# Loading the projection's weight units from GpSimd's queue, and clearing the inverse's operand on VectorE

## The chip, the cores and the metric

The kernel runs on one core of a Trainium2 chip. The metric is the device time of one execution in microseconds (us); lower is better. The engines are called as in the profile: PE (TensorE, with PEld for its weight loads), DVE (VectorE), ACT (ScalarE), POOL (GpSimd), SP (SyncE, which here only issues DMAs).

## The reference

One layer of a hybrid decoder over 1024 tokens of width 1024, in float32:

```
x = x + 0.5 * swiglu(rms_norm(x))                     # width 2816
h = rms_norm(x);  proj = h @ w_in                     # all projections of the mixer
q, k, v = silu(causal_dwconv(proj[qkv]))              # 8 heads of 128
o_gdn   = rms_norm(gated_delta_rule(q, k, v, g, beta)) * silu(z)
o_ssm   = rms_norm(ssd_scan(...) * silu(z))           # 16 heads of 64
x = x + concat(o_gdn, o_ssm) @ w_out
x = x + 0.5 * swiglu(rms_norm(x));  return rms_norm(x)
```

The gated delta rule works on chunks of the tokens. For each chunk it needs the inverse of a unit lower triangular matrix, I + tril(beta * k k^T * decay), and then steps a 128x128 state through the chunks, head by head.

## The kernel before

All large products are made of float32 numbers split into a rounded part (hi) and a rest (lo), three matmuls for each product: hi*hi, hi*lo and lo*hi, on tiles of 128x128 by 128x512. Most of them also go through a scheme of seven products for a 2x2 block product, in place of eight.

The program runs through the first feed-forward block, the norm, the state-space heads, the eight delta-rule heads, the output projection, and the second feed-forward block. The change lies in the delta-rule heads. Heads 0 to 3 take their projections of q, k, v and z as plain products (`proj_half`). Heads 4 to 7 take them from the scheme of seven products: `chunk` computes two projections of 128 columns for all 1024 tokens from seven weight units, two chunks per head, 8 chunks and 56 units in all. The constant `NESTED = 4` is where the first kind ends, so there are four heads of the second kind.

A weight unit is a tile of 128 partitions x 2 (hi, lo) x 512 float32, 512 KB. The units were computed during the first feed-forward block and stored in DRAM, in `wu_scr`. `first_units` makes four slots in SBUF and loads the first four units; `unit_prod` uses the next unit for twelve matmuls (L1260, L1261, L1262) and then calls `unit_load` for the unit four places on, which goes to the slot just used. That load (L1251) must wait until PE has finished with the slot.

Beside the chunks, each head goes through its own chain:

- `decays` (L1361 to L1370) loads the head's decay row, broadcast over the partitions, from `g_scr` to `dt` (L1365); ACT takes an exponential for `qe` (L1366); POOL masks `dt` causally with an affine select (`causal`, L970); ACT takes eight exponentials of `dt` (L1369).
- `k_part` transposes k on PE (L1346) and makes `kd` and the norms on ACT (L1350, L1355).
- PE multiplies k by k and k by q (L1443, L1444), DVE makes `u` and `dt` of it (L1447, L1450), and `u`'s diagonal 32x32 blocks go to DRAM (L1459) and come back as `fu`, one block per partition row (L1486).
- `token_sums` sums q's squares over the channels on PE (L978), copies the row on ACT (L981) and stores it (L983). Its tile `row` has the same buffer as `fx`.
- `fx` starts as the identity, cleared and set on POOL (L1490, L1492). DVE inverts the blocks by 31 steps of two instructions (L1496, L1498).
- `fx` goes to DRAM (L1501) and back (L1508, L1509). DVE transposes it (L1510), and small matmuls (L1516 to L1542) join the 32x32 blocks to 64x64 and 128x128. For that, the operand `x64` needs a zero block of 32 partitions x 8 x 32 numbers (L1527); the rest of it is written by ACT (L1528 to L1530). `x64` lies in the buffer of `fu`, so it can be written only after the last of the 31 steps.
- The recurrence over the 8 blocks of tokens (L1549 to L1576), the norm (L1582 to L1587), and the store to `mix_scr` (L1588).

The source is written with tiles, and the tool that builds the program adds the waits and decides in which order each engine and each DMA queue gets its instructions, from estimates of when each will be ready. So the trace shows one head's recurrence among the next head's unit products, and the source's order is not that of the trace. Each engine, and each queue, then works in that fixed order, so an instruction that waits holds those behind it.

At the end of the last head, POOL's queue also loads the first operands of the output projection (`out_start`, L1233 and L1234) and stores z (L1428).

Of the kernel before, what the change touches and what calls it, by code (L numbers as in the profile page):

```python
# [11 lines left out]
F32 = mybir.dt.float32  # L12
# [32 lines left out]
def kernel(  # L45
# [6 lines left out]
    nc = tc.nc  # L52
    V, A, G, T = nc.vector, nc.scalar, nc.gpsimd, nc.tensor
# [20 lines left out]
    wu_scr = [dram.tile([P, 7, 2, 512], F32, name=f"wu_scr{i}") for i in range(2 * (GH - 4))]  # L74
# [1171 lines left out]
    def unit_load(s):  # L1246

        if s < 7 * len(wu_scr):
            c, i = divmod(s, 7)
            u = slots[s % 4]  # L1250
            nc.sync.dma_start(out=u.bitcast(F32), in_=wu_scr[c][:, i])  # L1251
            units.append((s, u))

    def unit_prod(bank, m, first):

        s, u = units.pop(0)
        bh, bl = H_IN[m]
        for k in range(4):
            wh, wl = (u[:, i, k * P:(k + 1) * P] for i in range(2))
            T.matmul(bank, lhsT=wh, rhs=bh[k], start=first and k == 0, stop=False, skip_group_check=True)  # L1260
            T.matmul(bank, lhsT=wh, rhs=bl[k], start=False, stop=False, skip_group_check=True)  # L1261
            T.matmul(bank, lhsT=wl, rhs=bh[k], start=False, stop=k == 3, skip_group_check=True)  # L1262
        unit_load(s + 4)
# [48 lines left out]
    def first_units():  # L1312

        for i in range(2):
            t = wp.tile([P, 2, 2, 512], F32R, name="wunits", tag="wst")
            slots.extend(t[:, j] for j in range(2))
        for s in range(4):
            unit_load(s)
# [15 lines left out]
    with ExitStack() as cg:  # L1334
# [37 lines left out]
        for h in range(GH):  # L1372
# [63 lines left out]
            u = g2.tile([P, NB, P], F32, name="u")  # L1436
# [68 lines left out]
            x64, mt2 = lv2[0:64, 0], lv2[:, 1]  # L1505
# [18 lines left out]
                T.matmul(px[64:96, ls], lhsT=mt[96:128, b], rhs=xd[96:128, b], start=True, stop=True)  # L1524
                T.matmul(px[32:64, ls], lhsT=xd[32:64, b], rhs=mt[32:64, b], start=True, stop=True)
            pxv = px[:, 0:256].rearrange("p (b l) -> p b l", b=NB)
            G.memset(x64[0:32, :, 32:64], 0.0)  # L1527
            A.copy(out=x64[0:32, :, 0:32], in_=xtr[0:32])  # L1528
            A.copy(out=x64[32:64, :, 32:64], in_=xtr[32:64])
            A.mul(out=x64[32:64, :, 0:32], in_=pxv[32:64], mul=-1.0)  # L1530
# [227 lines left out]
```

## Time and profile before

| | |
|---|---|
| median of three runs | 2296.49 us (2296.11 to 2296.8) |
| profiled execution | 2296.6 us, of which 2294.9 is the span of the profile |
| granted clock of PE | 0.998 of full speed |
| PE busy | 2257.9 us, 98% of the span |
| DVE, ACT, POOL busy | 76%, 51%, 2% |
| weight units: loaded | 1105.7 to 1409.4 us, 56 loads of 512 KB from SP's queue |
| weight units: multiplied | 1183.2 to 1420 us |

A row of a stretch gives the busy time of each engine in it. A row of waits has the waiting engine, the line that waits, what ended the wait, the total in us, how often, and the longest. SPq and POOLq are the sequencers of the two engines that issue DMAs. In a timeline, the numbers in front are the start from the beginning of the span and the time it took, in us; in brackets stands the idle time of the engine before it and what ended that.

### The profile page before, as it was taken

Reading aid. Unit: us, or ns where it says so; the run is one execution under the profiler, and the core shown is the slowest. Engines: PE = TensorE matmul, PEld = TensorE weight load, DVE = VectorE, ACT = ScalarE, POOL = GpSimd, SP = SyncE. Lnnn points to the kernel's source line nnn. Section 1 sums busy time; section 2 is a strip of 40 time slices with the busy share of each in tenths; the row PEclk is TensorE's granted clock in tenths of the full one; section 3 lists DMA queues with packets and bytes.
Section 4 is the critical chain, followed back from the end, with each engine's and each line's share of the span. In section 5 each row is a group of like instructions: output and inputs, shape, how many; then the busy total and the mean of one; then the engine's idle time right before and its main releaser. Section 6 shows DMA issues by size and latency. Waiting matters only on the chain.

```text
span 2294.9 us, 31984 instructions
## 1 busy us (share of the span) xinstructions
PE 2257.9 (98%) x11654; PEld 1842.1 (80%) x11654; DVE 1751.5 (76%) x3225; ACT 1178.9 (51%) x2276; POOL 52.1 (2%) x118
## 2 busy tenths in 40 slices
PE   7999999999999999999999999999999999999998
PEld 5788888888878878888887777788878888888886
DVE  7989987769776887667667777778688676766787
ACT  7444433354366986875755566523543333334344
POOL 0000000000000110100000000000000000000000
PEclk9999999999999999999999999999999999999999
DMA  3467663497654433242356566436123232329446
GB/s 112 137 217 256 230 214 114 166 333 228 206 180 137 134 120 101 74 132 65 84 158 183 166 175 195 136 99 220 65 88 133 92 119 88 120 89 347 143 151 215
DMA packets 262194, 356.96 MB, mean 156 GB/s; under 512 B 60808, under 2 KB 167404, under 8 KB 260244
## 3 DMA queue, kind: packets, MB, share of 16 engines
q1 hardware_dynamic: 261220, 352.20, 47.2%
q0 software_dynamic: 816, 2.72, 0.3%
q8 instruction: 91, 1.49, 0.3%
q14 instruction: 67, 0.55, 0.1%
HBM read 249.34 MB, written 105.52 MB: 155 GB/s over the span
## 4 chain that ended last, share of the span: by engine, by line
PE 87%; ACT 6%; DVE 5%; issue 1%; DMA 1%; POOL 0%; SPq 0%; DVEq 0%; POOLq 0%; ACTq 0%
PE ps_pj L125 7%; PE ps_pj L123 7%; PE ps_pj L124 7%; PE ps_pj L335 6%; PE ps_pj L334 6%; PE ps_pj L336 6%; PE ps_mx L334 3%; PE ps_mx L336 3%; PE ps_mx L335 3%; PE ps_pj L564 2%; PE ps_pj L565 2%; PE ps_pj L563 2%; PE ps_pj L1260 2%; PE ps_oo L335 2%; PE ps_pj L1261 2%; PE ps_oo L334 2%
## 5 line engine op out<-in xcount | busy, mean ns | idle before, releaser
L336 PE MATMUL ps_pj<-bh,al 128*128 128x512 f32 x688 | 268.1, 390 | 0.0
L335 PE MATMUL ps_pj<-bl,ah 128*128 128x512 f32 x688 | 267.9, 389 | 0.0
L334 PE MATMUL ps_pj<-bh,ah 128*128 128x512 f32 x688 | 267.7, 390 | 0.0
L123 PE MATMUL ps_pj<-hhi,whi 128*128 128x512 f32 x576 | 229.4, 398 | 0.4 <-ACT gsb L901 0.4
L125 PE MATMUL ps_pj<-hhi,wlo 128*128 128x512 f32 x576 | 229.4, 398 | 0.0
L124 PE MATMUL ps_pj<-hlo,whi 128*128 128x512 f32 x576 | 228.3, 396 | 0.0
L336 PEld LDWEIGHTS ps_pj<-bh,al 128*128 128x128 f32 x688 | 129.2, 188 | 26.7
L335 PEld LDWEIGHTS ps_pj<-bl,ah 128*128 128x128 f32 x688 | 129.2, 188 | 26.6
L334 PEld LDWEIGHTS ps_pj<-bh,ah 128*128 128x128 f32 x688 | 129.0, 188 | 26.7
L317 DVE TENSOR_TENSOR as<-wst 128x512 f32<-128x512 f32 x220 | 144.3, 685 | 2.1 <-DMA wst<-in_ffn_w_up_dram 2.0
L241 ACT CAST hid<-hraw 128x1024 fp32r<-128x1024 f32 (+1 forms) x84 | 82.2, 980 | 123.9 <-PE ps_oo L565 46.3
L241 ACT CAST ah<-wst 128x512 fp32r<-128x512 f32 x88 | 54.5, 621 | 176.4 <-PE ps_oo L335 113.4
L242 DVE TENSOR_TENSOR al<-as,ah 128x512 fp32r<-128x512 f32 x220 | 141.1, 685 | 4.8 <-ACT ah L241 4.3
L334 PE MATMUL ps_mx<-bh,ah 128*128 128x512 f32 x352 | 138.6, 396 | 3.9 <-ACT m L343 1.3
L335 PE MATMUL ps_mx<-bl,ah 128*128 128x512 f32 x352 | 138.3, 393 | 0.5 <-DVE bl L242 0.5
L336 PE MATMUL ps_mx<-bh,al 128*128 128x512 f32 x352 | 137.8, 391 | 0.3 <-DVE al L242 0.3
L241 ACT CAST ah<-as 128x512 fp32r<-128x512 f32 x220 | 125.1, 618 | 24.1 <-DVE as L317 24.1
L125 PEld LDWEIGHTS ps_pj<-hhi,wlo 128*128 128x128 f32 x576 | 108.3, 188 | 21.9 <-issue 0.9
L123 PEld LDWEIGHTS ps_pj<-hhi,whi 128*128 128x128 f32 x576 | 108.4, 188 | 21.8 <-ACT gsb L901 0.8
L124 PEld LDWEIGHTS ps_pj<-hlo,whi 128*128 128x128 f32 x576 | 108.4, 188 | 21.1 <-issue 0.8
L242 DVE TENSOR_TENSOR hid<-hraw,hid 128x1024 fp32r<-128x1024 f32 (+1 forms) x84 | 95.0, 1131 | 26.3 <-ACT hid L241 26.1
L343 ACT COPY m<-ps_pj 128x512 f32<-128x512 f32 x88 | 51.4, 587 | 111.7 <-PE ps_pj L336 111.4
(505 smaller groups left out, 5635.4 us busy)
## 6 DMA issues: line engine op xcount, KB each, us to landing
hraw<-hid_scr SPq DMA_DIRECT2D x70, 512.0 KB, 3.9
wu_scr<-wunit SPq DMA_DIRECT2D x112, 256.0 KB, 3.6
wunits<-wu_scr SPq DMA_DIRECT2D x56, 512.0 KB, 3.8
hid_scr<-hs SPq DMA_DIRECT2D x110, 256.0 KB, 2.9
wst<-in_ffn_w_down_dram SPq DMA_DIRECT2D x50, 512.0 KB, 4.7
wst<-in_ffn_w_gate_dram SPq DMA_DIRECT2D x22, 1024.0 KB, 6.0
wst<-in_ffn_w_up_dram SPq DMA_DIRECT2D x22, 1024.0 KB, 6.0
hid_scr<-sg SPq DMA_DIRECT2D x44, 256.0 KB, 2.0
```

What stands on the lines that cost most here:

```text
L123: T.matmul(o, lhsT=wh, rhs=mh, start=first, stop=False)
L124: T.matmul(o, lhsT=wh, rhs=ml, start=False, stop=False)
L125: return T.matmul(o, lhsT=wl, rhs=mh, start=False, stop=last)
L241: return (A.copy(out=hi, in_=src), V.tensor_tensor(out=lo, in0=src, in1=hi.bitcast(F32), op=ALU.subtract))
L242: V.tensor_tensor(out=lo, in0=src, in1=hi.bitcast(F32), op=ALU.subtract))
L317: V.tensor_tensor(out=t, in0=v[0], in1=v[1], op=v[2])
L334: T.matmul(bank, lhsT=wh[:, k], rhs=bh[:, k], start=a, stop=False, skip_group_check=True)
L335: T.matmul(bank, lhsT=wh[:, k], rhs=bl[:, k], start=False, stop=False, skip_group_check=True)
L336: T.matmul(bank, lhsT=wl[:, k], rhs=bh[:, k], start=False, stop=z, skip_group_check=True)
L343: A.copy(out=t, in_=bank)
L563: T.matmul(bank, lhsT=hh, rhs=wh, start=first and k == 0, stop=False, skip_group_check=True)
L564: T.matmul(bank, lhsT=hh, rhs=wl, start=False, stop=False, skip_group_check=True)
```

## The change

Two lines. The load of a weight unit is issued by GpSimd (`G`) in place of SyncE, and the zero block of `x64` is written by VectorE (`V`) in place of GpSimd. Nothing else in the source differs.

```
@@ unit_load
             u = slots[s % 4]
-            nc.sync.dma_start(out=u.bitcast(F32), in_=wu_scr[c][:, i])
+            G.dma_start(out=u.bitcast(F32), in_=wu_scr[c][:, i])
             units.append((s, u))
@@ the head's inverse, L1527
             pxv = px[:, 0:256].rearrange("p (b l) -> p b l", b=NB)
-            G.memset(x64[0:32, :, 32:64], 0.0)
+            V.memset(x64[0:32, :, 32:64], 0.0)
             A.copy(out=x64[0:32, :, 0:32], in_=xtr[0:32])
```

More of the change, by code (lines that the diff above doesn't have):

```diff
@@ L1250, in unit_load @@
             u = slots[s % 4]
-            nc.sync.dma_start(out=u.bitcast(F32), in_=wu_scr[c][:, i])
+            G.dma_start(out=u.bitcast(F32), in_=wu_scr[c][:, i])
             units.append((s, u))
@@ L1526 @@
             pxv = px[:, 0:256].rearrange("p (b l) -> p b l", b=NB)
-            G.memset(x64[0:32, :, 32:64], 0.0)
+            V.memset(x64[0:32, :, 32:64], 0.0)
             A.copy(out=x64[0:32, :, 0:32], in_=xtr[0:32])
```

## The prediction

> **What bounds the kernel now.** I read the page first, its engine totals and the chain that ended last, and then the table of stretches for the place that the change touches.
>
> ```profile
> span 2294.9 us, 31984 instructions
> ...
> PE 2257.9 (98%) x11654; PEld 1842.1 (80%) x11654; DVE 1751.5 (76%) x3225; ACT 1178.9 (51%) x2276; POOL 52.1 (2%) x118
> ...
> PE 87%; ACT 6%; DVE 5%; issue 1%; DMA 1%; POOL 0%; SPq 0%; DVEq 0%; POOLq 0%; ACTq 0%
> ```
>
> ```profile
> 1183.00:1420.00 237.00, 235.84 (x1637) 186.49 (x1635) 168.73 (x546) 140.36 (x398) 8.64 (x29) 1.00 0.61 182
> 1420.00:1440.00 20.00, 17.71 (x77) 13.21 (x76) 14.70 (x23) 19.02 (x38) 2.69 (x3) 1.00 0.40 117
> ```
>
> PE is 87% of the chain that ended last, and SP's and POOL's queues are 0%. In the stretches the columns are the stretch, its length, and the busy time of PE, PEld, DVE, ACT and POOL, then the granted clock (full). The weight units are multiplied from 1183 to 1420. PE idles there for 237.00 - 235.84 = 1.16 us and for 2.29 us in the next 20. The change can win back 3.45 us of idle PE before 1440, no more, unless it also alters how densely PE works while it counts as busy. Who ends this idle time stands in the list of waits of PE, for 1183 to 1460:
>
> ```profile
> PE ps_pj L123 <- ACT xa L1220: 2.3, 2, 2.0
> PE ps_mx L1443 <- ACT kd L1355: 0.8, 2, 0.4
> PE ps_sc L1516 <- DVE lv L1510: 0.2, 1, 0.2
> ```
>
> None of the three is a weight unit, and none is the memset of L1527.
>
> **Part 1: 56 loads leave SP's queue.** SP is often late with them. The waits of SP's queue, 1090 to 1530:
>
> ```profile
> SPq L1251 <- PE ps_pj L1262: 57.0, 21, 6.7
> SPq L1365 <- PE ps_oo L1565: 41.3, 5, 20.5
> SPq L1588 <- ACT vr L1587: 32.2, 6, 19.9
> SPq L1501 <- DVE fx L1498: 28.0, 7, 8.1
> SPq L1251 <- PE ps_pj L1260: 22.2, 6, 4.8
> SPq L983 <- ACT row L981: 20.0, 4, 6.8
> ```
>
> L1251 is the unit load, which waits for the products that still read its slot. The other rows name their own data: the store L1501 waits for fx itself, L983 for its row. So they would not go out sooner with the loads out of the way, and freeing SP gives nothing on them. What does get late is a load behind L983. The worst place that I found, in order of time:
>
> ```profile
> 1320.51 0.55 SPq L983 DMA_DIRECT2D row_scr<-row  x1
> 1321.15 0.39 SPq L1251 DMA_DIRECT2D wunits<-wu_scr  x1
> ```
>
> ```profile
> 1328.94 0.40 PE L1260 MATMUL ps_pj<-hhi,wunits 128*128 128x512 f32 x1
> ```
>
> This product is the first to read the load of 1321.15 (the 34th of 56; units are used in order, twelve products each). Between them are 7.79 us. From issue to landing:
>
> ```profile
> wunits<-wu_scr SPq DMA_DIRECT2D x56, 512.0 KB, 3.8
> ...
> z_scr<-zc SPq DMA_DIRECT2D x7, 512.0 KB, 2.6
> ...
> nat<-ssm_scr SPq DMA_DIRECT2D x3, 1024.0 KB, 4.9
> ...
> y<-ssm_scr POOLq DMA_DIRECT2D x1, 1024.0 KB, 6.0
> x<-in_w_out_dram POOLq DMA_DIRECT2D x1, 1024.0 KB, 10.1
> z_scr<-zc POOLq DMA_DIRECT2D x1, 512.0 KB, 5.2
> ```
>
> 7.79 - 3.8 leaves 3.99 us to spare even there. Loads that go out on time have much the same, where the products of units run back to back, as in these two first products of neighbouring units:
>
> ```profile
> 1295.35 0.39 PE L1260 MATMUL ps_pj<-hhi,wunits 128*128 128x512 f32 x1
> ...
> 1298.08 0.39 PE L1260 MATMUL ps_pj<-t,wunits 128*128 128x512 f32 x1
> ```
>
> A unit takes 2.73 us. With four slots, three units lie between a slot's release and its next use, 8.2 us, and 8.2 - 3.8 is 4.4. So about 4 us is the least, and coming sooner saves zero.
>
> **Part 2: the same loads enter POOL's queue.** Their landing gets slower. From one kind of buffer (ssm_scr, 1024 KB), POOL needs 6.0 and SP 4.9 us, +1.1; for the store of z it is 5.2 against 2.6, +2.6. Those are the two ends, 4.9 and 6.4 us for a unit; I take +1.1, since y is a load from DRAM as the units are. The spare time of 4.0 becomes 2.9 (1.4 at the far end), so PE does not wait. If a load came later than that, PE would stand for the difference, because its products run in a written order.
>
> What is POOL's issue worth, and what waits behind it? The rows of POOL's timeline:
>
> ```profile
> 1298.01 1.09 POOL L970 TENSOR_SCALAR_AFFINE_SELECT dt<-dt 128x1024 f32<-128x1024 f32 x1 [34.24 <-ACT qe L1366]
> ...
> 1322.27 0.32 POOL L1490 MEMSET fx<- 128x256 f32 x1 [20.67 <-DMA row_scr<-row]
> 1322.65 0.58 POOL L1492 MEMSET fx<- 32x8 f32 x4
> ...
> 1405.22 0.58 POOL L1234 DMA_DIRECT2D y<-ssm_scr  x1 [22.37 <-PE ps_oo L1565]
> ```
>
> A load costs POOL about 0.58 us (y), 56 of them 32 us, on an engine that is 8.64 us busy in those 237: room is there. The order is what matters. Three things of POOL are in the way of loads or the other way round. (a) The clearing of fx, L1490, waits for row_scr to land, since the row lies in the same buffer; a load queued behind it goes out at 1322.65 + 0.58 = 1323.2, against 1321.15 now if it is that same load. 3.99 - 2.1 - 1.1 = 0.8 us is then left; at the +2.6 end PE would stand 0.7 us. (b) y and x, from 1405 on, stand ahead of the last loads and fill the queue with 2 MB; in bytes the total is that of before, and the last unit has always shared the engines with them. I take zero, with 0 to 2 us. (c) The causal mask L970 may stand behind a load. That is a wait which before could not exist, and it is the chain of the head: ACT waits for the mask before its eight exponentials.
>
> ```profile
> 1299.13 2.45 ACT L1369 ACTIVATE dt<-dt,ngc 128x128 f32<-128x128 f32 x8 [1.24 <-POOL dt L970]
> ```
>
> Behind the exponentials ACT makes kd, and PE's L1443 is the one that waits for it (0.8 us in two times, above). So that chain has no slack, and whatever the mask loses, PE loses. A load that is due costs the mask its 0.58 us. I put in one such, in one of the three heads whose masks fall among the loads: +0.6 us. The ends are 0 and rival A's price.
>
> **Part 3: the memset goes from POOL to VectorE.**
>
> ```profile
> L1527 POOL MEMSET lv<- 32x256 f32 x8 | 2.4, 302 | 96.8 <-DVE ft L1496 94.6 <-DMA wunits<-wu_scr 2.2
> ```
>
> ```profile
> L1519 DVE COPY lv<-ps_sc x16: 417/424/431, 1064.8 to 1518.1; 32x256 f32<-32x256 f32 x16
> ```
>
> ```profile
> 1301.27 0.17 DVE L1498 TENSOR_TENSOR fx<-fx,ft 128x8 f32<-128x8 f32 x1
> 1301.36 0.68 DVE L1270 TENSOR_TENSOR zc<-ps_pj,zc 128x512 f32<-128x512 f32 x1
> 1302.67 1.29 DVE L847 SCALAR_TENSOR_TENSOR vt__11963<-pre,cols,vt__11963 128x1024 f32<-128x1024 f32 x1 [0.63 <-ACT vt__11963 L1293]
> ```
>
> On POOL it takes 0.30 us; DVE's copy of the same size takes 0.42, which bounds it above. Eight of them are 2.4 to 3.4 us of DVE. It must come behind the last step of fx (1301.27 here), and 0.7 us later DVE itself stands for 0.63 us waiting for ACT, so it is covered. Without that cover 0.4 us in each of the four later heads would fall on u and the next inverse, 1.7 us in all. I take 0. For POOL the removal matters: this memset waits for DVE (94.6 us in all) and would have held the loads.
>
> **The sum.** Against the profiled execution, span 2294.9 and time 2296.6: 0 (SP) + 0 (landing) + 0.6 (mask) + 0 (memset) = 2297.2; its time is 0.1 above the median of the three runs (2296.49), so against that median 2297.1 us. That is within 0.2%, 4.6 us, about the least that a measurement of this kernel can tell from no change.
>
> [...] Two rows of VectorE's timeline:
>
> ```profile
> 1298.13 1.00 DVE L1498 TENSOR_TENSOR fx<-fx,ft 128x24 f32<-128x24 f32 x1
> ...
> 1405.70 0.22 DVE L1498 TENSOR_TENSOR fx<-fx,ft 128x69 f32<-128x69 f32 x1
> ```
>
> The first, 24 elements wide, takes 1.00 us: it lies under the mask of 1298.01. The second, 69 wide, lies under the issue of y (1405.22 + 0.58) and takes 0.22. So POOL's mask holds DVE; a DMA issue does not, and I charge DVE nothing. [...]
>
> **The rivals.**
> A (slower): the queue order holds the mask. If a load stands ahead of it whose slot PE has not yet left, the mask waits for the rest of that unit and the issue. 2.73 us a unit plus 0.58 is 3.3 us per head; in two of the three heads 6.6, so 2303. It decides from the point where the held time passes 2.3 us a head in two heads. For it: the mask (1298.01) and the end of a unit (1298.08) coincide, so the order is a toss. Against: the list that orders the queues places an instruction when it is expected to be ready, which mostly puts a due mask first.
>
> [...]
>
> C (faster): the order changes for the better. Loads that come on time let the products be placed otherwise among the small matmuls:
>
> ```profile
> L1262 PE MATMUL ps_pj<-hhi,wunits 128*128 128x512 f32 x128 | 52.8, 413 | 0.0
> ```
>
> ```profile
> L565 PE MATMUL ps_pj<-wd,hid 128*128 128x512 f32 x37 | 14.5, 392 | 0.0
> ```
>
> The second is the same product away from the heads (600 to 700). 672 products at up to 21 ns are 14 us hidden in busy time. A fifth of it, 2.8, with two thirds of the 3.45 us of idle time, 2.3, gives 2291.4. Against: the switches between large and small matmuls are there in any order.
>
> D (the change does not do what it says): the loads are late as before, held by fx's clearing instead of L983. With 0.8 us to spare it costs nothing, 2296.5, and it is counted in the forecast.
>
> **How the numbers follow.** Forecast with D 0.60 (its own range 2293 to 2300: plus and minus the 3.45 us of idle time), A 0.20, B 0.03, C 0.17. Half of A's nominal cases lie under 2303. Low 2291 leaves out half of C, high 2303 half of A and B: together 0.20. Faster by over 0.2%: C, 0.17. Slower: A and B with 0.02 of the forecast's edge, 0.25. The rest, 0.58, is the same.
>
> **What would show it.** Right: PE idle from 1183 to 1440 between 2.5 and 5 us; L1251 under POOLq with landings near 5 us; SP's waits without L1251, yet L1501 and L1365 as long as now; PE's waits without wunits. Wrong: PE waiting for a DMA wunits<-wu_scr (landing or fx's clearing missed), the mask released by a load rather than by qe, or a stretch whose PE count per us has changed (C).

## The result and the profile after

The changed kernel takes 2317.66 us (median of 4 runs, 2316.76 to 2322.1); the kernel before, on the same chip, 2296.64 us. The ratio is 1.0094, with a 95% interval of 1.0076 to 1.0111: 21 us slower. The forecast was 2297.1 us, in a range that ended at 2303. The profiled execution took 2318.34 us, its span is 2316.6, 21.7 us more than before.

The page of the changed kernel: span, busy engines, and the chain that ended last.

```profile
span 2316.6 us, 31991 instructions
...
PE 2266.9 (98%) x11654; PEld 1850.2 (80%) x11654; DVE 1755.4 (76%) x3233; ACT 1183.3 (51%) x2280; POOL 77.9 (3%) x166
...
PE 74%; DVE 12%; ACT 6%; DMA 4%; issue 2%; SPq 1%; POOL 0%; DVEq 0%; ACTq 0%
```

POOL has 56 loads more to issue and is still nowhere on the chain. What moved there is VectorE: 5% before, 12% now, while PE fell from 87 to 74%. The stretches of the changed kernel (length, busy time of PE, PEld, DVE, ACT and POOL, then granted clock, DMA share, GB/s):

```profile
1183.00:1420.00 237.00, 227.43 (x1592) 180.51 (x1591) 158.84 (x490) 132.61 (x383) 32.83 (x74) 0.99 0.57 162
1420.00:1440.00 20.00, 16.94 (x76) 13.24 (x75) 18.98 (x66) 17.67 (x32) 3.40 (x5) 1.00 0.89 316
1440.00:1460.00 20.00, 18.53 (x150) 14.45 (x149) 13.14 (x27) 16.78 (x35) 0.56 (x1) 0.91 0.35 96
```

PE's idle time from 1183 to 1460 was 3.44 us and is 9.57 + 3.06 + 1.47 = 14.1. And the granted clock, 1.00 there before, is below 1: in three spells (stretches of the clock's record at half of full speed), of 6.83, 3.41 and 10.24 us, PE gets half of it. So there are 10.7 us more of idle time, and PE is busy for 3.79 + 3.41 + 10.24 = 17.4 us of those spells, which costs half of that, 8.7 us (in the second spell, successive 128x512 products of L123 to L125 start 0.43 us apart, just ahead of it 0.23). Together 19.4 us. Against its own matmuls in the trace of before, PE falls back by 18.6 us between 1187 and 1552, so these two account for the loss in this stretch. The rest of the 21.7 us is mostly a lag of 2.9 us that this trace has already at 1187, ahead of the stretch; other traces are there between 1.0 us ahead of before (sp_new_order below, in the same new order) and 2.6 us behind it. The waits of PE from 1183 to 1460, those of 0.9 us and more:

```profile
PE ps_pj L1260 <- DVE pre L1270: 7.2, 2, 5.6
PE ps_pj L124 <- DVE w L242: 2.0, 1, 2.0
PE ps_sc L1516 <- DVE lv L1510: 1.3, 2, 0.8
PE ps_sc L1523 <- DVE lv L1519: 0.9, 1, 0.9
PE ps_pj L123 <- DVE zc L1270: 0.9, 1, 0.9
```

No weight unit is among them. PE waits for VectorE, in lines that the change does not touch. The largest wait is one stall of 5.6 us. ScalarE, VectorE and PE ahead of it in the changed kernel, in their own timelines:

```profile
1227.37 2.45 ACT L1369 ACTIVATE dt<-dt,ngc 128x128 f32<-128x128 f32 x8 [0.23 <-POOL dt L970]
1229.72 1.14 ACT L1293 ACTIVATE kt<-pre,cols 128x1024 f32<-128x1024 f32 x1
...
1239.81 0.59 ACT L1279 COPY pre<-ps_pj 128x512 f32<-128x512 f32 x1 [7.44 <-DVE fx L1498]
```

```profile
1233.29 1.28 DVE L847 SCALAR_TENSOR_TENSOR kt<-pre,cols,kt 128x1024 f32<-128x1024 f32 x1
...
1238.42 1.28 DVE L847 SCALAR_TENSOR_TENSOR kt<-pre,cols,kt 128x1024 f32<-128x1024 f32 x1
...
1239.96 1.15 DVE L847 SCALAR_TENSOR_TENSOR qt<-pre,cols,qt 128x1024 f32<-128x1024 f32 x1
1241.04 0.67 DVE L1270 TENSOR_TENSOR pre<-ps_pj,zc 128x512 f32<-128x512 f32 x1
```

```profile
1241.76 0.79 PE L1260 MATMUL ps_pj<-t,wunits 128*128 128x512 f32 x1 [5.63 <-DVE pre L1270]
```

Read it backwards. PE's product goes into a buffer of `ps_pj` that VectorE's addition L1270 has to read first (1241.04), and stood 5.63 us for that. That addition writes `pre`, which the last of the key's three convolution steps, L847, still reads until 1238.42 + 1.28 = 1239.70 (ScalarE's copy L1279, which also writes `pre`, starts then too; its row names the fx step beside it). And in VectorE's order the addition stands behind the last step of the query as well (1239.96), so it starts at 1241.04. These six steps come last among VectorE's steps of the inverse. Their first input, L1293, comes on ScalarE behind eight exponentials, but it is done at 1230.86, 2.4 us before the first of them, so it is VectorE's own order that holds them. The same instructions in the kernel before:

```profile
1220.78 1.15 ACT L1293 ACTIVATE kt<-pre,cols 128x1024 f32<-128x1024 f32 x1 [3.13 <-DVE pre L1270]
```

```profile
1222.20 1.28 DVE L847 SCALAR_TENSOR_TENSOR kt<-pre,cols,kt 128x1024 f32<-128x1024 f32 x1
```

L1293 stood 9 us earlier there, ahead of L1587, and L847 11 us earlier, among the inverse's steps (2.9 us of each are the lag of the whole trace). What differs is the order that the tool which builds the program wrote for ScalarE, VectorE and PE. The first differences are small: on ScalarE near 1123 us `kd` (L1355) goes behind two copies (L1528, L1529), on VectorE near 1209 us L1471 goes ahead of L1556. From there much of four heads is laid out otherwise: with the two traces aligned from 1100 to about 1620 us, some 315 of VectorE's 1021 instructions, 168 of ScalarE's 726 and 755 of PE's 3327 stand elsewhere, while PE's first 6254 matmuls (to 1228 us) keep their order. That the tool's estimates shift with the loads on another queue is an inference; the estimates are not on record.

### The profile page after: what moved, and what is told of

Same layout as the page of the kernel before. It is cut to its first block, busy times and chain, and to the rows that moved or that the text cites. A ratio compares the mean times of both kernels' runs of the same rounds, so it can differ in the third digit from the quotient of the medians.

```text
span 2316.6 us, 31991 instructions
## 1 busy us (share of the span) xinstructions
PE 2266.9 (98%) x11654; PEld 1850.2 (80%) x11654; DVE 1755.4 (76%) x3233; ACT 1183.3 (51%) x2280; POOL 77.9 (3%) x166
## 4 chain that ended last, share of the span: by engine, by line
PE 74%; DVE 12%; ACT 6%; DMA 4%; issue 2%; SPq 1%; POOL 0%; DVEq 0%; ACTq 0%
PE ps_pj L125 6%; PE ps_pj L124 6%; PE ps_pj L123 6%; PE ps_pj L334 6%; PE ps_pj L336 6%; PE ps_pj L335 6%; PE ps_mx L334 3%; PE ps_mx L336 3%; PE ps_mx L335 3%; PE ps_oo L334 2%; PE ps_oo L336 2%; PE ps_oo L335 2%; PE ps_pj L564 1%; PE ps_pj L565 1%; DMA wst<-in_ffn_w_down_dram 1%
## 5 line engine op out<-in xcount | busy, mean ns | idle before, releaser
L123 PE MATMUL ps_pj<-hhi,whi 128*128 128x512 f32 x576 | 229.4, 398 | 0.7 <-ACT pre L1392 0.4
L125 PE MATMUL ps_pj<-hhi,wlo 128*128 128x512 f32 x576 | 229.2, 398 | 0.0
L123 PEld LDWEIGHTS ps_pj<-hhi,whi 128*128 128x128 f32 x576 | 108.3, 188 | 22.6 <-ACT gsb L901 0.8
L125 PEld LDWEIGHTS ps_pj<-hhi,wlo 128*128 128x128 f32 x576 | 108.3, 188 | 21.9 <-issue 0.9
```

Of the source, the lines that this page charges most:

```text
L123: T.matmul(o, lhsT=wh, rhs=mh, start=first, stop=False)
L125: return T.matmul(o, lhsT=wl, rhs=mh, start=False, stop=last)
```

## Experiments

Theory: the *order* costs the time. Moving the loads made the builder write another one, it stalls PE on VectorE, and the stalls pull the clock down. Rivals: the queue itself costs it (GpSimd's issue and landing), or the clearing on VectorE does. Ratios are to the kernel before on the same chip, with 95% intervals. The last columns compare the profiled execution with that of before (span 2294.9): what the span grew, and how much idle time of PE and half of the time at half clock grew between 1183 and 1500 us, summed from the matmul and clock records. The kernel before ran at 2298.72 us beside the first four runs below the changed kernel, at 2297.48 and 2299.06 beside the next three and the last three, against 2296.64 in the result; expectations in us are to be read with that.

| run | loads | order | median us | ratio | span | idle | clock |
|---|---|---|---|---|---|---|---|
| changed kernel | POOL | new | 2317.66 | 1.0094 [1.0076, 1.0111] | +21.7 | +10.7 | +10.2 |
| load_only | POOL | new | 2318.11 | 1.0079 [1.0056, 1.0101] | +26.1 | +11.1 | +17.1 |
| memset_only | SP | before's | 2300.84 | 1.0006 [0.9996, 1.0016] | -0.4 | +0.3 | 0 |
| pool_old_order | POOL | before's | 2301.23 | 1.0012 [1.0003, 1.0022] | +1.0 | +0.8 | 0 |
| sp_new_order | SP | new | 2314.64 | 1.0063 [1.0045, 1.0080] | +16.5 | +9.0 | +12.0 |
| after_old_order | POOL | before's | 2301.68 | 1.0018 [1.0009, 1.0026] | +10.5 | +2.3 | +6.8 |
| after_taps_early | POOL | new, 20 us of it as before | 2322.83 | 1.0109 [1.0095, 1.0124] | +22.3 | +11.8 | +12.0 |
| before_taps_late | SP | before's, 20 us of it new | 2305.35 | 1.0035 [1.0023, 1.0047] | +6.5 | +5.7 | +1.7 |
| pe_old_order | POOL | before's on PE alone | 2315.88 | 1.0087 [1.0062, 1.0112] | +20.1 | +11.8 | +5.1 |
| dve_act_old_order | POOL | before's on DVE and ACT alone | 2302.24 | 1.0015 [1.0005, 1.0024] | +4.7 | +2.0 | +1.7 |
| act_loads | ACT | a fourth one | 2321.56 | 1.0115 [1.0082, 1.0147] | +22.3 | +15.3 | +8.5 |

Idle time and clock add up to the growth of the span within 5 us in every row (the worst is sp_new_order, 21.0 for 16.5). The column of the clock counts idle time in a spell a second time. With half of PE's busy time in the spells in its place, the two come within 2.3 us of what PE falls back by between 1187 and 1552 in every row (19.9 for 19.0 in sp_new_order).

**Each half of the change alone.** The diffs are its two lines, one at a time.

> The kernel before with the unit loads on GpSimd's queue, and the clearing left on GpSimd. The written order of TensorE, ScalarE and SyncE is that of the changed kernel, instruction for instruction. Order theory (the move of the load makes the program builder write another order for TensorE, VectorE and ScalarE, and that order stalls TensorE): 2316 to 2320 us, PE idle of about 14 us between 1183 and 1460 us, the stall of about 5.6 us ahead of a product of L1260 near 1236 us, three more half-clock spells. Queue theory (GpSimd's queue itself costs it): about 2317 us too. Clearing theory (the eight clears on VectorE cost it): 2296 to 2298 us.

> The kernel before with the clearing alone on VectorE (8 instructions of 0.27 us); the loads stay on SyncE, and TensorE, ScalarE and SyncE keep before's order. Order theory and queue theory: 2295.5 to 2298 us, no more than 8 x 0.27 = 2.2 us above before. Clearing theory: 2317 us.

The load carries all of it (2318.11 us; idle 13.1 us between 1183 and 1460, a first stall of 5.5 us, four spells at half clock in place of the three expected). The clearing alone ran at 2300.84 us, above the 2295.5 to 2298 expected, but so did the kernel before in these rounds: it is 2.1 us over that, with an interval that includes zero, and PE's order is that of before. The clearing theory is dead; order and queue are still together.

**Queue and order taken apart.** Edges of issue order between successive instructions of one engine, with no wait in them, hold PE, VectorE, ScalarE and SyncE to a given order through the nested heads (a cut from the added lines, shortened where the dots stand):

```
+def hold_order(nc, tc):
+    at = {i.name: i for i in nc.cur_bb.bb.instructions}
+    for row in ...:                     # one engine's order, by the numbers of the traced instructions
+        ...
+        tc.add_manual_dep(ins, prev.name, mybir.DependencyInfo(
+            mybir.DependencyClass.NoSync, mybir.DependencyReason.DATA), reason="held order")
```

> The unit loads on GpSimd's queue and the clearing on GpSimd, as in the run with the load alone, but the order in which TensorE, VectorE, ScalarE and SyncE issue their instructions through the nested heads is held to that of the kernel before (edges of issue order only, no waits). Order theory: 2294 to 2299 us, PE idle between 1183 and 1460 us near 3.5 us, one half-clock spell near 1681 us and the one at the end. Queue theory: about 2317 us.

> The unit loads on SyncE's queue and the clearing on GpSimd, as before, but TensorE, VectorE and ScalarE (and SyncE's other transfers) issue in the order of the changed kernel through the nested heads. Order theory: 2314 to 2322 us, with the stall of about 5.6 us near 1236 us and the extra half-clock spells of the changed kernel. Queue theory: 2296 to 2299 us.

With the loads on GpSimd in before's order, all 11654 matmuls come in the order of before, and PE's waits from 1183 to 1460 are those of before:

```profile
PE ps_pj L123 <- ACT xa L1220: 2.9, 2, 2.0
PE ps_mx L1443 <- ACT kd L1355: 0.7, 2, 0.4
PE ps_sc L1516 <- DVE lv L1510: 0.2, 1, 0.2
```

With the loads still on SyncE and the clearing on GpSimd, but in the new order, they are those of the changed kernel:

```profile
PE ps_pj L1260 <- DVE pre L1270: 6.5, 2, 5.0
PE ps_pj L124 <- DVE w L242: 2.1, 1, 2.1
PE ps_sc L1523 <- DVE lv L1519: 0.9, 1, 0.9
```

So the order costs the time without the queue (+0.63%), and the queue without the order costs 0.12%, barely off zero. Its 2301.23 us are 2 us above what I expected (2294 to 2299) and 2.5 above the kernel before in these rounds. Where those lie stays open: its trace, from the fastest of its ten runs, shows 1.0 us more of span and 0.8 of idle time. The sum of the two is 0.75%, under the 0.94% of the whole change, but the intervals are too wide to say whether anything is left.

**The whole change in the old order.** The changed kernel with before's order held in the same way.

> The whole change (unit loads on GpSimd's queue, clearing on VectorE), with TensorE, VectorE, ScalarE and SyncE held to the order of the kernel before through the nested heads. Order theory: 2295 to 2300 us, at most 0.2% from before; PE idle of 3.4 to 4.5 us between 1183 and 1460 us, no extra half-clock spell. If queue and clearing cost something only together: above 2302 us.

2301.68 us, 0.18% over before: within the 0.2%, a little above the microseconds that I expected (the kernel before ran 0.8 us higher here than at the result), and just under the 2302 from which I would have said that queue and clearing cost something together. PE's idle time between 1183 and 1460 is 5.8 us, above the 3.4 to 4.5 expected. Its profiled execution was the slowest of its 12 (2307.16, the fastest 2298.06) and has a spell of 13.65 us at half clock that was not expected; the section on the hardware shows what stands ahead of it.

**Where in the order?** First the 20 us around the largest stall: in the changed kernel, the instructions read above go back to where before has them, and the converse. PE keeps the order of the kernel that each is made from. The moves, in short (`+` marks what goes ahead; taps are the steps of the convolution):

```
 ACT: +L1293 kt, L1587 x8, L1366, +L1293 qt, +L1274, L1369 x8     (taps early; taps late is the reverse)
 DVE: the six L847 and two L1270 among the fx steps of 1224 to 1235, not behind those of 1233 to 1241
```

> The changed kernel with its own order, except in one stretch of 20 us (1222 to 1242): ScalarE's first step of the key's and the query's convolution (L1293) goes ahead of L1587 and L1369, and VectorE's six convolution steps (L847) and two additions (L1270) go where the kernel before has them among the inverse's steps. Stall-and-clock theory (the late steps make the 5.6 us stall, and the stall makes the half-clock spell behind it): the stall near 1236 us falls below 1 us, the spell of 6.8 us at half clock goes with it, in all 5 to 9 us less than the changed kernel: 2309 to 2313 us. If the clock falls for another reason: the stall goes and the spell stays, 2312 to 2314 us. If the stall only moves to a later wait: 2316 to 2318 us.

> The converse: the kernel before, loads on SyncE and clearing on GpSimd, its own order but for the same stretch, in which ScalarE's L1293 and VectorE's convolution steps and additions come as late as in the changed kernel. Stall-and-clock theory: a stall of 5 to 9 us ahead of a product of L1260 near 1233 us and a half-clock spell of 3.4 to 6.8 us behind it: 2303 to 2310 us. If the late steps are not the cause, or other order hides them: 2296 to 2299 us.

Taps late, two stalls of PE appear in before's order:

```profile
1230.42 0.50 PE L1260 MATMUL ps_pj<-hhi,wunits 128*128 128x512 f32 x1 [2.21 <-ACT zc L1274]
1238.95 0.67 PE L1260 MATMUL ps_pj<-t,wunits 128*128 128x512 f32 x1 [3.24 <-DVE pre L1270]
```

They are 5.5 us, and with a spell of 3.41 us at half clock behind them the run is 0.35% slower, as that theory had it. So the late steps are enough to stall PE. But taking them back does not mend the changed kernel:

```profile
1242.25 0.50 PE L1260 MATMUL ps_pj<-t,wunits 128*128 128x512 f32 x1 [1.88 <-DVE zc L1270]
1251.91 0.26 PE L1516 MATMUL ps_sc<-lv,u 32*32 32x32 f32 x1 [5.77 <-DVE lv L1510]
```

The 5.6 us are gone and 1.88 + 5.77 us stand in their place. L1516 needs the inverse, whose last step, L1498, is followed by a store and loads through DRAM before VectorE can transpose it:

```profile
1240.09 0.17 DVE L1498 TENSOR_TENSOR fx<-fx,ft 128x8 f32<-128x8 f32 x1
...
1251.41 0.45 DVE L1510 STREAM_TRANSPOSE lv<-lv 128x256 f32<-128x256 f32 x1 [6.05 <-DMA lv<-fs_x]
```

That way takes 11.2 us here (1251.41 - 1240.26) and 12.0 in the kernel before, and what hides it is unit products on PE. The stretches from the last step to L1510, of unit products alone (first row before, second row taps early; busy time of PE, of PEld, in the second also of POOL's load issues):

```profile
1241.16:1253.14 11.98, 8.42 (x33) 5.59 (x33) 1.00 0.61 162
```

```profile
1240.26:1251.41 11.15, 3.12 (x13) 2.18 (x12) 1.05 (x2) 1.00 0.66 162
```

Where the kernel before has 33 products for that time, the mended order has 13 left, since PE's new order works off the others ahead of it. In the changed kernel as it is, the stall at 1236 had put off products of just that kind: 33 of them run in the 11.2 us behind its last step. My own theory expected 2309 to 2313 us and fell; the rival that the stall only moves was right, and at 2322.83 even above its figure. A local repair is not enough.

So the next pair asks which engines' order matters over the whole stretch.

> The whole change, with TensorE alone held to the order of the kernel before through the nested heads; VectorE, ScalarE and SyncE as the program builder then writes them (a third order, neither before's nor the changed kernel's). If TensorE's order is what stalls (its unit products spent early, none left beside VectorE's run): 2297 to 2304 us, idle between 1183 and 1460 us below 7 us. If VectorE's and ScalarE's order is: above 2308 us. If only an order of all engines made together is good: above 2308 us here and in the next run.

> The whole change, with VectorE and ScalarE held to the order of the kernel before through the nested heads; TensorE and SyncE as the program builder then writes them. If TensorE's order is what stalls: above 2308 us. If VectorE's and ScalarE's order is: 2297 to 2304 us, idle between 1183 and 1460 us below 7 us. If only an order made together is good: above 2308 us.

PE alone in before's order leaves the stalls, with VectorE's and ScalarE's new order:

```profile
PE ps_pj L1260 <- DVE pre L1270: 4.0, 1, 4.0
PE ps_pj L124 <- DVE w L242: 2.7, 2, 2.0
PE ps_mx L1443 <- ACT kd L1355: 2.4, 3, 1.5
```

VectorE and ScalarE in before's order take them away, with an order of PE that neither kernel has:

```profile
PE ps_pj L123 <- ACT xa L1220: 3.1, 2, 2.5
PE ps_sc L1516 <- DVE lv L1510: 0.9, 2, 0.7
```

2315.88 against 2302.24 us. In the slow one some 198 of VectorE's 1021 instructions from 1100 to about 1620 us stand elsewhere than in before, and PE's stand as in before up to 1498 us; in the fast one some 600 of PE's 3327 matmuls stand elsewhere and VectorE's and ScalarE's none. PE, 98% busy, is the engine that loses the time, but what loses it is the order of VectorE and ScalarE. (Those two were held together; which of them it is was not tried.)

The new order also gives ScalarE more ACT_TABLE_LOAD instructions, of 1.28 us each: 18 between 1090 and 1460 us, where before has 14. They are not what costs the time, since the run with PE alone held has 14 too.

**Another queue.** One line, the loads on ScalarE's queue, nothing held.

```
-            nc.sync.dma_start(out=u.bitcast(F32), in_=wu_scr[c][:, i])
+            A.dma_start(out=u.bitcast(F32), in_=wu_scr[c][:, i])
```

> The kernel before with the unit loads on ScalarE's queue instead (clearing on GpSimd); nothing held, so the program builder writes a fourth order. Order theory: the time goes with the stalls of that order and not with the queue, and can come out anywhere from 2294 to 2325 us; TensorE's idle time plus half of the time at half clock, from 1183 to 1500 us, accounts for its distance to before within 4 us. If a load on another queue than SyncE's costs the time by itself: 2313 to 2322 us, with TensorE waiting for the units.

Again slower by 1.15%, again with other stalls of PE, on VectorE for the most part:

```profile
PE ps_sc L1516 <- DVE lv L1510: 7.2, 3, 3.9
PE ps_mx L1443 <- DVE dt L1450: 2.1, 1, 2.1
PE ps_pj L123 <- ACT xa L1220: 1.5, 1, 1.5
```

Idle time and clock add up to 23.8 us for 22.3 us of span, within the 4 us expected. The profile names a weight unit as what PE waited for once, for 0.7 us, so late units are not the cause. Whether ScalarE's queue costs something beside the order was not tried. No order that the builder wrote anew for VectorE and ScalarE came near before's: 2317.66, 2315.88 and 2321.56 us. No version tried beats the kernel before.

## Why the prediction was wrong, step by step

*Part 1, SP's queue, 0.* Right. L1251 has left SP, and PE gained nothing by it: in before's order, its idle time with the loads off SP is 4.3 us against 3.4 (pool_old_order, 1183 to 1460). SP's waits, 1090 to 1530, after:

```profile
SPq L1365 <- PE ps_oo L1565: 88.9, 5, 24.3
SPq L1501 <- DVE fx L1498: 57.9, 7, 14.9
SPq L1588 <- ACT vr L1587: 37.4, 5, 13.3
```

They are longer than the 41.3, 28.0 and 32.2 of before, because SP comes to each sooner and stands there until the same data is ready. In before's order they are longer still for L1365 and L1588 (119.3 and 45.6, and 57.4 for L1501, in pool_old_order), so it is not the new order that does it. My sign that they would stay as long as before was wrong; a longer wait of a queue is here a freer queue.

*Part 2, landing, 0.* Right for nearly all, and pessimistic in the middle: 4.2 us from issue to landing, not 4.9 to 6.4.

```profile
wunits<-wu_scr POOLq DMA_DIRECT2D x56, 512.0 KB, 4.2
```

The tight ones took 4.5 to 5.2 us, and but for the last two the least time to spare was 2.6 us, near the 2.9 forecast. The 55th load, in flight together with y and x, is the exception: it landed 7.4 us after its issue, and its first product started 0.14 us after that, 0.1 us late. In the run with the load alone the same unit took 8.3 us, and PE stood 0.96 us for it (the profile names L1496 there, but the wait ended with the landing). In sp_new_order, with the loads on SP, it took 8.5 us and PE stood 0.45 us, so this is not a price of POOL's queue. It was inside the 0 to 2 us that I allowed for y and x.

*The mask, +0.6* (rival A: 3.3 us a head). A's mechanism did occur, at about a third of its size, in two of the heads. ScalarE and POOL in one of them, after:

```profile
1291.50 1.06 ACT L1366 ACTIVATE qe<-dt 128x1024 f32<-128x1024 f32 x1 [2.33 <-DMA dt<-g_scr]
```

```profile
1293.21 0.53 POOL L1251 DMA_DIRECT2D wunits<-wu_scr  x1 [2.19 <-PE ps_pj L1262]
1293.79 1.09 POOL L970 TENSOR_SCALAR_AFFINE_SELECT dt<-dt 128x1024 f32<-128x1024 f32 x1
```

The mask waits for qe, which is done at 1292.56; before, it starts 0.12 us after qe. Here a load stands ahead of it that has to wait until PE has left its slot (1293.21), and with the issue of 0.53 us the mask starts 1.23 us after qe. So it loses 1.1 us here, 1.3 us in the head before (1224.79 and 1226.24), 0.6 us in the third, and 0.4 us in the last, there behind the load of x. It costs ScalarE next to nothing, and that is luck: ScalarE's new order has L1587 and L1293 ahead of the exponentials, which wait for the mask in one of these heads alone, 0.23 us (the row of 1227.37 above). With before's order held, all four masks start about 0.1 us after qe in both runs with the loads on POOL, so there the term is 0.

*Rival B*, which has 0.03 of the chances and a part of the range, stood for VectorE holding up POOL's issues. No run shows such a hold: the 56 issues took 0.53 to 0.58 us each. *Part 3, the memset, 0*: eight of 0.27 us, and nothing waits for them; alone 1.0006 [0.9996, 1.0016].

*The step that failed* is the sum itself: it added four terms at an order of PE, VectorE and ScalarE taken as given. The prediction said "The order is what matters", and asked that of POOL's queue alone. That the order of other engines could change stood only in rival C, "the order changes for the better", at 0.17. The same mechanism with the other sign had no rival and no price, though the bound is lopsided: a new order could win back 3.45 us of idle time and a part of 14 us hidden in busy time, and could lose without such a limit. What it did: the new order alone, with before's queue, measures +0.63%, 16 us by the medians. With the order held to before's, the whole change measures +0.18% [0.09, 0.26], 4.2 us, where the four terms add up to 0.6. So the terms have the right size, a few microseconds and not twenty, but they are some 3 us short, and no run says which of them is; the mask, put at 0.6, is not seen to cost anything there. What failed for the other 16 us is the frame. The sign that I had given for being wrong, "a stretch whose PE count per us has changed", is what happened (x1592 for x1637 from 1183 to 1420).

*A second omission*: idle time was priced at its own length. Here 10.7 us more of it came with another 8.7 us lost at half clock.

## What to carry to other kernels

Where a tool orders the instructions from estimates, an edit of one DMA's queue can be an edit of every engine's order, as it was here; the other line, which moved the memset to VectorE, left it alone. So compare the two built orders engine by engine before pricing the lines of the diff, and if they differ, hold the old order and time the change alone. Give a redrawn order a price and a rival of its own, with the bad sign too: all three orders that the tool wrote anew for VectorE and ScalarE lost here, 17 to 23 us, though three are too few for a rule. And price a stall of the matmul engine above its length when it is packed into a few microseconds, because here the clock followed (8.7 us lost at half clock beside 10.7 us more of idle time).

## What the runs showed of the hardware

In these traces the clock falls after a few microseconds of thin work, and it took no long pause: PE busy for 2.04 of 3.41 us, with no pause over 0.92 us, was followed by half clock (1457.18 below). In the stretches of the changed kernel around the first and the third of its three spells, the number behind the length is PE's busy time, and the third from the end is the clock:

```profile
1235.31:1238.72 3.41, 0.82 (x4) 0.36 (x2) 3.41 (x7) 0.00 (x0) 1.05 (x2) 1.00 0.28 64
1238.72:1245.55 6.83, 3.79 (x9) 3.01 (x10) 4.81 (x7) 3.87 (x4) 0.00 (x0) 0.50 0.48 150
...
1457.18:1460.59 3.41, 2.04 (x60) 1.57 (x54) 3.19 (x6) 3.35 (x9) 0.00 (x0) 1.00 0.73 291
1460.59:1470.83 10.24, 10.24 (x58) 8.84 (x58) 4.80 (x17) 4.78 (x8) 0.00 (x0) 0.50 0.30 104
```

Within a trace all spells start on one grid of 3.41 us, and all last a whole number of such steps, but for the one that the end of the program cuts (the changed kernel's three start at 1238.73, 1440.12 and 1460.60 us, 59 and 6 steps apart, and last 2, 1 and 3 steps). I cut the eleven traces that have a spell between 1000 and 2250 us on that grid and took PE's busy share of each step that ran at full clock. Of 25 steps with a share of at most 0.53, 22 were followed by half clock; of the steps of large products with 0.54 to 0.75, none; and of steps with many small matmuls (43 to 83 matmuls) and 0.60 to 0.64, five of five. The longest single pause in a step that was followed by half clock was as short as 0.92 us (the wait of L1523 above) among small matmuls and 1.08 us among large ones. These limits were read off after the event, and no run was made to test them.

The place of the grid may also account for part of the scatter. The same pause of 1.96 us of before (PE, near 1438) falls across two steps in its trace and costs no clock, and within one in the old-order run of the whole change, where 13.65 us at half clock follow:

```profile
1435.80:1439.21 3.41, 2.02 (x9) 1.31 (x7) 3.41 (x5) 3.41 (x8) 0.00 (x0) 1.00 0.38 58
1439.21:1442.62 3.41, 2.85 (x45) 2.34 (x45) 1.98 (x6) 3.37 (x12) 0.00 (x0) 1.00 0.74 184
```

```profile
1441.87:1445.28 3.41, 1.45 (x10) 1.04 (x9) 2.69 (x6) 3.41 (x13) 0.00 (x0) 1.00 0.77 219
1445.28:1458.93 13.65, 13.65 (x127) 10.68 (x126) 6.38 (x21) 6.49 (x14) 0.00 (x0) 0.50 0.27 105
```

Where the grid lies differs from trace to trace, with no pattern that these runs show, and this kernel, which has such pauses, varied by 8.2 us: of 19 runs of the kernel before on one chip, the fastest (2295.19 us) had a mean granted clock of 0.999, the slowest (2303.41) 0.996, and over the 19 the longer time goes with the lower clock (correlation -0.88).
